# Sums of weight forms and channels from GpSimd to VectorE, and value stores from GpSimd's DMA queue to ScalarE's

## The chip, the cores and the metric

The kernel runs on one core of one Trainium2 chip. The metric is the time of one execution on the device in microseconds (us). The core has five engines that run their own instruction queues side by side: TensorE (PE in the profile; its weight loads are PEld), VectorE (DVE), ScalarE (ACT), GpSimd (POOL) and SyncE (SP), which here only issues DMA transfers. DMA transfers can be issued from the queues of SyncE, ScalarE and GpSimd; in this kernel nearly all come from SyncE.

## The reference

One layer of a streaming encoder works on two groups with the same weights: a prompt of 2048 frames and a sample of 32 frames, each frame 1024 channels wide, all in float32.

```python
h = rmsnorm(x, g_pre_mix)
z = h @ w_in                               # 1024 -> 2560: pool u | q | f | i | g
y_pool = pool_mix(u_ext, ...)              # trailing means over 2/4/8/16 frames, a map per group
q = silu(zq); fgate = lb + (1 - lb) * sigmoid(zf); kin = (1 - lb) * sigmoid(-zf)
S1, o = hgrn_run(S0, q, kin, zi, log(fgate))   # gated recurrence, 4 heads, chunks
y_hg = rmsnorm(o, g_hg_norm) * silu(zg)
x = x + rmsnorm(concat(y_pool, y_hg) @ w_out, g_post_mix)
h2 = rmsnorm(x, g_pre_ffn)
f = (silu(h2 @ w_gate) * (h2 @ w_up)) @ w_down   # 1024 -> 2816 -> 1024
x = x + rmsnorm(f, g_post_ffn)
```

The outputs are the new frames of both groups, the last 15 pooling rows and the recurrence's states.

## The kernel before, in words

The prompt is worked in two halves of 1024 frames (`halves[0]` and `halves[1]`; `S.B` is true for the second). For each half come the values (columns `i` of `w_in`), the other columns with the recurrence and the pooling windows, the projection by `w_out` (`project`), and the gate and up products (`gate_up`). The down products of both halves stand at the end (`down`).

Matmuls are exact to float32 by splitting. Every operand is stored as a rounded upper part (`hi`, float32r, by a ScalarE copy) and a lower part (`lo`, the difference, by a VectorE subtraction), and a product is three matmuls: hi by hi, hi by lo, lo by hi. Large products are also blocked 2x2 with seven products in place of eight. So each operand needs sums and differences of its blocks, called forms, before the split. The products are numbered 1 to 7; products 1 and 2 and 4 use plain blocks, and 5, 6, 7 and 3 use sums.

`weight_forms` makes the forms of the weights that the second half's columns use. It runs while TensorE works on the first half's gate and up products. For each of eight pairs of column blocks it loads four blocks (`weight_block`, tile `wb`, 128x512), makes four sums and differences on GpSimd, and splits four of the results (`put`): the upper part on ScalarE (line 464), the lower part on GpSimd (line 465), then two stores to the DRAM tile `wd` on SyncE's queue. `front_pairs` loads them back for the second half (line 929), three products ahead.

`second_channels` prepares the second half's channels: scaled inputs (line 575), their upper and lower parts (lines 577 to 581), and then block sums on 128x1024 tiles (line 373, the helper `sums`): `b12`, `t2s`, `b11` and `b21`, two tiles each. `t2s` is on VectorE, the three others on GpSimd.

`values` computes the second half's values into eight PSUM banks. Each is copied out to a tile `vt`, even ones by ScalarE and odd ones by VectorE (line 809), and stored to the DRAM tile `vd` from GpSimd's queue (line 810). The recurrence loads a head's part later (line 1192).

Right after the values comes `front_pairs`. For each pair, products 1, 2, 6, 7, 5, 4, 3 run in this order (banks `gx`, `gz`, `gy`). Product 1 is copied out by ScalarE (line 956), products 6, 5 and 3 accumulate further into the same bank `gx`, and line 967 copies the bank out between products 6 and 5, so product 5 must wait for that copy. `use` (lines 857 to 873) applies the sigmoids on ScalarE into tiles `sg` (lines 864, 868) and the products on VectorE. Line 956 is the first ScalarE instruction of a pair; 864 and 868 of `use` come ahead of 967 in the program.

What sets the order: the program is written out in full, and TensorE's order is the program's. Side work (weight forms, channels, recurrence) is written as generators, `Task`s. A `yield` of so many nanoseconds says how much planned TensorE time (`Pace.t`, added up by `mm`, line 205) must pass before the task's next step is put into the program, at the next `poll`, which stands after every third matmul of a product. `finish` puts all remaining steps at once; `second_start` calls it for the weight forms, eleven products before the end of the first half's gate and up, and then begins the second half's loads. On the other four engines a planner orders the instructions when the kernel is built, by its own costs and by program order as priority. Each engine then runs its queue strictly in order.

Tiles come from rotating pools. `t2` tiles (128x512) share 25 slots among all these stages: `wb`, `fhi`, `flo`, `vt`, `sg`, `wf`, `hhi`, `hlo`, `c11` and others. A new tile's first writer waits until the slot's former tile has been read for the last time, which for a stored tile means that the store has landed.

Of the kernel before, what the change touches and what calls it, by code (L numbers as in the profile page):

```python
# [13 lines left out]
ALU = mybir.AluOpType  # L14
# [20 lines left out]
T1 = 2000.0  # L35
Y0 = 18000.0
Y1 = 8000.0
FORMS = 8000.0
LOOKRAW = 2
SLOT = HALF  # L40
CHUNK = 128
# [43 lines left out]
def body(tc, ins, outs, cst):  # L85
    nc = tc.nc
    ctx = ExitStack()
    with ctx:
# [9 lines left out]
        def ztile(name, shape=None, dt=F32):  # L98
            return UP.tile(shape or [P, SLOT], dt, tag="u", name=name)

        def xtile(name, shape=None):
            return UP.tile(shape or [P, SLOT], F32R, tag="u", name=name)

        def mmbank(name="mmb"):
            return MM.tile([P, 512], F32, tag="mm", name=name)

        def axbank(name="axb"):
            return AX.tile([P, 512], F32, tag="ax", name=name)
# [4 lines left out]
        def t2(name, shape=None, dt=F32):  # L113
            return TP.tile(shape or [P, 512], dt, tag="t", name=name)
# [94 lines left out]
        def rcost(n):  # L209
            return max(107.0, n / 2.4 + 2.5)  # L210
# [74 lines left out]
        def ahead(n):  # L285
            its = Stream.items
            raws(n + LOOKRAW)
            while Stream.nsplit < min(n, len(its)):
                i = Stream.nsplit
                its[i] = split(its[i], Stream.wide[i])  # L290
                Stream.nsplit += 1

        def take(look=LOOK):
            i = Stream.used
            Stream.used += 1
            ahead(i + 1 + look)
            r = Stream.items[i]
            Stream.items[i] = None
            return r

        def in_turn(trios):

            for a, b in ((0, 2), (0, 3), (1, 2)) if len(trios) > 1 else ((0, 2), (1, 2), (0, 3)):
                for t in trios:
                    yield t[a], t[b]
# [57 lines left out]
        def form(src):  # L363
            hl = [(xtile("fhi", [P, D]), xtile("flo", [P, D])) for _ in src]
            for r, (hi, lo) in zip(src, hl):
                nc.scalar.copy(hi, r)
            for r, (hi, lo) in zip(src, hl):
                nc.vector.tensor_tensor(lo, r, hi.bitcast(F32), ALU.subtract)
            return hl

        def sums(dst, a, b, op, eng=nc.vector):
            for d, x, y in zip(dst, a, b):
                eng.tensor_tensor(d, x, y, op)
# [66 lines left out]
        vd = DP.tile([NH, P, NCH, P], F32, name="vd")  # L440
# [12 lines left out]
        def weight_block(n, m, kh):  # L453
            kind, h = PAIRS[n][m]
            c0 = COLS[kind] + h * P
            t = t2("wb", [P, 4, P])
            nc.sync.dma_start(out=t, in_=w_in[kh * 512:kh * 512 + 512, c0:c0 + P].rearrange("(k p) c -> p k c", p=P))
            return t.rearrange("p k c -> p (k c)")

        def weight_forms():  # L460

            def put(n, p, src):
                hi, lo = t2("fhi", dt=F32R), t2("flo", dt=F32R)
                nc.scalar.copy(hi, src)
                v.tensor_tensor(lo, src, hi.bitcast(F32), ALU.subtract)
                for i, t in enumerate((hi, lo)):
                    nc.sync.dma_start(out=wd[n][p - 1, :, i, :], in_=t.bitcast(F32))

            v = nc.gpsimd
            for n in range(len(PAIRS)):  # L470
                a21, a22 = weight_block(n, 1, 0), weight_block(n, 1, 1)
                yield FORMS
                v.tensor_tensor(a22, a21, a22, ALU.add)
                a11 = weight_block(n, 0, 0)
                yield FORMS
                put(n, 5, a22)
                v.tensor_tensor(a21, a11, a21, ALU.subtract)
                v.tensor_tensor(a11, a22, a11, ALU.subtract)
                a12 = weight_block(n, 0, 1)
                yield FORMS  # L480
                put(n, 7, a21)
                v.tensor_tensor(a12, a12, a11, ALU.subtract)
                yield FORMS
                put(n, 6, a11)
                yield FORMS
                put(n, 3, a12)

        class Half:
            pass
# [58 lines left out]
        def channel_loads(S):  # L548

            for tg in range(2):  # L550
                S.rb[tg] = t2("rb")
                nc.sync.dma_start(out=S.rb[tg], in_=roots[0:1, tg * 512:tg * 512 + 512].broadcast_to([P, 512]))
            S.xT = [[None] * 4 for _ in range(2)]
            for kp in range(2):
                channel_pair(S, kp)

        def channel_pair(S, kp):
            for tg in range(2):
                x = S.xT[tg][kp] = ztile("xT", [P, 2, 512])
                t0 = S.tok0 + tg * 512  # L560
                nc.sync.dma_start(out=x, in_=x_t[:, 2 * kp:2 * kp + 2, t0:t0 + 512])
            raws(Stream.used + kp + 1)

        def second_channels(S):

            channel_loads(S)
            yield Y0
            for kp in range(4):
                for tg in range(2):
                    x, rb = S.xT[tg][kp], S.rb[tg]  # L570
                    hi, lo = xtile("fhi", [P, D]), xtile("flo", [P, D])
                    parts = [slice(0, 512), slice(512, 1024)] if kp == 0 else [slice(0, 1024)]
                    S.xT[tg][kp] = flat = x.rearrange("p k t -> p (k t)")
                    for i in range(2):
                        nc.vector.scalar_tensor_tensor(x[:, i], x[:, i], g_pre[:, 2 * kp + i:2 * kp + i + 1], rb, ALU.mult, ALU.mult)
                        if kp == 0:
                            nc.scalar.copy(hi[:, parts[i]], flat[:, parts[i]])
                    if kp:
                        nc.scalar.copy(hi, flat)
                    for cs in parts:  # L580
                        nc.vector.tensor_tensor(lo[:, cs], flat[:, cs], hi[:, cs].bitcast(F32), ALU.subtract)
                    S.plain[tg].append((hi, lo))
                    if kp == 0 and tg == 0:
                        ahead(Stream.used + 1)
                S.seen[0] = 2 * kp + 2
                if kp < 2:
                    channel_pair(S, kp + 2)
                yield Y1
            b11, b21 = S.xT[0][0:2], S.xT[0][2:4]
            b12, b22 = S.xT[1][0:2], S.xT[1][2:4]  # L590
            S.F[1], S.F[2], S.F[3] = S.plain[0][0:2], S.plain[0][2:4], S.plain[1][2:4]
            sums(b12, b12, b11, ALU.subtract, nc.gpsimd)
            yield T1
            t2s = [ztile("t2s", [P, D]) for _ in range(2)]
            sums(t2s, b22, b12, ALU.subtract)
            yield 2000.0
            S.F[6] = form(t2s)
            sums(b11, t2s, b11, ALU.subtract, nc.gpsimd)
            yield 3000.0
            sums(b21, b21, t2s, ALU.subtract, nc.gpsimd)  # L600
            S.F[7] = form(b11)
            yield 3000.0
            S.F[5] = form(b12)
            yield 3000.0
            S.F[4] = form(b21)
# [186 lines left out]
        def values(S, pairs):  # L792
            pss = [mmbank("vps") for _ in range(4)] + [axbank("vps") for _ in range(4)]
            for k in range(0, KD, 2):
                _, hi, lo = take(1)
                while S.seen[0] < k + 2:
                    S.norm.step()
                if k == 4:
                    next(pairs)
                for i in range(8):  # L800
                    c0 = i % 4 * P
                    trios = [(*(x[:, kk * 512 + c0:kk * 512 + c0 + P] for x in S.plain[i // 4][k // 2]), hi[kk], lo[kk]) for kk in range(2)]
                    for n, (a, b) in enumerate(in_turn(trios)):
                        mm(pss[i], a, b, k == 0 and n == 0, k + 2 == KD and n == 5, rcost(512))
                        if n % 3 == 2:
                            poll()
                    if k + 2 == KD:
                        vt = t2("vt", [P, NH, P])
                        (nc.vector.tensor_copy if i % 2 else nc.scalar.copy)(vt, pss[i].rearrange("p (h c) -> p h c", c=P))
                        nc.gpsimd.dma_start(out=vd[:, :, i, :].rearrange("h p c -> p h c"), in_=vt)  # L810
            Smp.mix = Task(sample_mix(), 4000.0)

        def sample_values():
# [1301 lines left out]
```

## Time and profile before

| what | value |
|---|---|
| median of 3 runs | 2081.92 us (2081.21 to 2084.04) |
| the profiled execution's own time | 2080.79 us |
| its span, first to last instruction | 2079.0 us |
| mean granted TensorE clock | 0.995 |
| TensorE busy | 2050.9 us, 99% |
| VectorE busy | 1464.9 us, 70% |
| ScalarE busy | 850.8 us, 41% |
| GpSimd busy | 413.9 us, 20% |
| DMA | 389.15 MB, 187 GB/s on average |

The profile gives each instruction's start and duration on its engine, by line, operation and tile. A row of the lists of waits reads: engine, tile and line that waited, what ended the wait, the sum of the waits in us, how many, and the longest. In a timeline a bracket gives the engine's idle time ahead of an instruction and what ended it; "xN" is the number of instructions merged in the row. "Issue" there means that nothing which the profile shows ended the wait. Idle time of an engine other than the one that sets the end costs nothing by itself.

### The profile page before, as it was taken

How to read it: one execution, taken by the hardware profiler on the slowest of the kernel's cores; microseconds unless marked ns; L12 is line 12 of the kernel's file. 1: busy time of each engine (PE TensorE's matmuls, PEld its weight loads, DVE VectorE, ACT ScalarE, POOL GpSimd, SP SyncE). 2: the span in 40 equal slices, each digit the busy share in tenths (PEclk: the TensorE clock that was granted, in tenths of full speed). 3: DMA queues.
4: the chain of work that ended last, by engine and by line, in shares of the span. 5: the costliest groups of instructions: out<-in, count | busy, mean ns of one | idle time of the engine just before them, and what ended most of it. 6: DMA issues, size and time to landing. Idle time of an engine off the chain costs nothing.

```text
span 2079.0 us, 34579 instructions
## 1 busy us (share of the span) xinstructions
PE 2050.9 (99%) x12980; PEld 1669.0 (80%) x12980; DVE 1464.9 (70%) x2252; ACT 850.8 (41%) x1689; POOL 413.9 (20%) x484
## 2 busy tenths in 40 slices
PE   9999999999999999799999999999999999999998
PEld 8788888888888887678887788888888778888876
DVE  5555674799887888666676697776666766566587
ACT  6544344654554544333344563444444521011032
POOL 0223421212222221333242100000000210110134
PEclk9999999999999999899999999999999999999999
DMA  8633344537787778464573614554445797776779
GB/s 290 200 101 113 103 142 143 171 109 236 226 245 216 219 217 253 152 239 151 194 267 132 193 51 137 163 149 145 138 142 167 235 336 221 220 224 200 220 199 225
DMA packets 427672, 389.15 MB, mean 187 GB/s; under 512 B 22360, under 2 KB 324432, under 8 KB 427504
## 3 DMA queue, kind: packets, MB, share of 16 engines
q1 hardware_dynamic: 424288, 376.65, 57.7%
q0 software_dynamic: 2784, 9.70, 2.2%
q8 instruction: 103, 1.69, 0.3%
q14 instruction: 65, 0.53, 0.1%
q10 hardware_dynamic: 432, 0.57, 0.1%
HBM read 251.77 MB, written 135.07 MB: 186 GB/s over the span
## 4 chain that ended last, share of the span: by engine, by line
PE 93%; DVE 4%; issue 1%; ACT 1%; DMA 1%; POOL 1%; DVEq 0%; SPq 0%; ACTq 0%; POOLq 0%
PE gx L206 26%; PE gy L206 13%; PE dx L206 11%; PE ops L206 9%; PE mmb L206 8%; PE gz L206 6%; PE dy L206 5%; PE vps L206 4%; PE dz L206 3%; PE gb L206 1%; PE gw L206 1%; PE gsps L206 1%; PE tps L349 1%; PE ups L206 1%; DVE acc L1887 1%
## 5 line engine op out<-in xcount | busy, mean ns | idle before, releaser
L206 PE MATMUL gx<-fhi,wf 128*128 128x512 f32 x1632 | 464.5, 393 | 13.0 <-ACT c L967 11.4
L206 PEld LDWEIGHTS gx<-fhi,wf 128*128 128x128 f32 x1632 | 304.5, 188 | 78.6 <-ACT c L967 11.8
L206 PE MATMUL gx<-flo,wf 128*128 128x512 f32 x816 | 256.1, 393 | 0.0
L206 PE MATMUL gy<-fhi,wf 128*128 128x512 f32 x832 | 239.9, 391 | 1.0 <-DVE c L1709 1.0
L206 PE MATMUL dx<-dhi,hst 128*128 128x512 f32 x640 | 185.4, 391 | 0.8 <-DVE acc L1887 0.7
L206 PEld LDWEIGHTS gy<-fhi,wf 128*128 128x128 f32 x832 | 155.4, 188 | 33.4 <-ACT wf L1598 1.6
L206 PEld LDWEIGHTS gx<-flo,wf 128*128 128x128 f32 x816 | 153.8, 188 | 32.3
L1603 DVE TENSOR_TENSOR wf<-s,wf 128x512 fp32r<-128x512 f32 x176 | 136.7, 783 | 58.6 <-ACT wf L1598 57.1
L1887 DVE TENSOR_TENSOR acc<-dx,acc 128x512 f32<-128x512 f32 x168 | 115.0, 689 | 71.1 <-PE dx L206 70.2
L206 PEld LDWEIGHTS dx<-dhi,hst 128*128 128x128 f32 x640 | 119.6, 188 | 29.9 <-issue 3.4
L1598 ACT CAST wf<-s 128x512 fp32r<-128x512 f32 x176 | 107.0, 620 | 73.5 <-PE gy L206 17.4
L206 PE MATMUL gy<-flo,wf 128*128 128x512 f32 x416 | 131.1, 392 | 0.0
L1826 ACT CAST dhi<-t 128x1024 fp32r<-128x1024 f32 x20 | 20.6, 1054 | 252.8 <-DVE dlo L1827 183.9
L1813 POOL TENSOR_TENSOR t<-wdr 128x1024 f32<-128x1024 f32 (+1 forms) x6 | 13.4, 2226 | 514.3 <-DMA wdr<-in_w_down_dram 506.2
L1598 ACT CAST wf<-wraw 128x512 fp32r<-128x512 f32 x132 | 80.6, 621 | 79.2 <-PE gx L206 35.9
L206 PE MATMUL gz<-fhi,wf 128*128 128x512 f32 x384 | 112.5, 393 | 0.0
L1603 DVE TENSOR_TENSOR wf<-wraw,wf 128x512 fp32r<-128x512 f32 x132 | 94.4, 722 | 24.5 <-ACT wf L1598 24.3
L206 PE MATMUL dx<-dlo,hst 128*128 128x512 f32 x320 | 98.7, 390 | 0.0
L206 PE MATMUL dy<-dhi,hst 128*128 128x512 f32 x320 | 98.6, 389 | 0.0
L206 PEld LDWEIGHTS gy<-flo,wf 128*128 128x128 f32 x416 | 78.1, 188 | 16.9 <-issue 0.8
L206 PE MATMUL mmb<-hTlo,whi 128*128 128x512 f32 x256 | 90.1, 409 | 0.0
L1887 DVE TENSOR_TENSOR acc<-dy,acc 128x512 f32<-128x512 f32 x88 | 60.6, 689 | 38.6 <-PE dy L206 38.0
(381 smaller groups left out, 4153.2 us busy)
## 6 DMA issues: line engine op xcount, KB each, us to landing
hst<-hdFalse SPq DMA_DIRECT2D x140, 256.0 KB, 2.9
hst<-hdTrue SPq DMA_DIRECT2D x140, 256.0 KB, 3.6
wf<-wd SPq DMA_DIRECT2D x112, 256.0 KB, 5.1
wraw<-in_w_gate_dram SPq DMA_DIRECT2D x50, 512.0 KB, 4.3
wraw<-in_w_up_dram SPq DMA_DIRECT2D x50, 512.0 KB, 4.5
hdFalse<-hhi SPq DMA_DIRECT2D x77, 256.0 KB, 4.0
hdFalse<-hlo SPq DMA_DIRECT2D x77, 256.0 KB, 2.7
hdTrue<-hhi SPq DMA_DIRECT2D x77, 256.0 KB, 2.3
```

Of the source, the lines that this page charges most:

```text
L206: nc.tensor.matmul(out, l, r, start=start, stop=stop, skip_group_check=more)
L349: nc.tensor.transpose(ps[:, c:c + P], xn[:, (2 * kp + kk) * P:(2 * kp + kk + 1) * P], ident)
L1598: nc.scalar.copy(wf[:, 0], getattr(M, src) if isinstance(src, str) else src)
L1603: nc.vector.tensor_tensor(wf[:, 1], getattr(M, src) if isinstance(src, str) else src, wf[:, 0].bitcast(F32), ALU.subtract)
L1813: nc.gpsimd.tensor_tensor(W.t1, b12, b11, ALU.subtract)
L1826: nc.scalar.copy(hi, src)
L1887: nc.vector.tensor_tensor(dst, ps, dst, ALU.add)
```

## The change

Three things change, with no change in what is computed.

- In `weight_forms` the sums and the lower parts go from GpSimd to VectorE. `put` becomes a generator: it pauses 3000 ns between the upper part and the lower part with its stores. The pauses between the other steps go from 8000 to 5600 ns.
- In `second_channels` the three sums on GpSimd go to VectorE.
- In `values` the stores of `vt` to `vd` are issued from ScalarE's queue instead of GpSimd's.

```diff
-FORMS = 8000.0
+FORMS = 5600.0
...
             def put(n, p, src):
                 hi, lo = t2("fhi", dt=F32R), t2("flo", dt=F32R)
                 nc.scalar.copy(hi, src)
+                yield 3000.0
                 v.tensor_tensor(lo, src, hi.bitcast(F32), ALU.subtract)
                 for i, t in enumerate((hi, lo)):
                     nc.sync.dma_start(out=wd[n][p - 1, :, i, :], in_=t.bitcast(F32))
 
-            v = nc.gpsimd
+            v = nc.vector
...
-                put(n, 5, a22)
+                yield from put(n, 5, a22)
...
-                put(n, 7, a21)
+                yield from put(n, 7, a21)
...
-                put(n, 6, a11)
+                yield from put(n, 6, a11)
...
-                put(n, 3, a12)
+                yield from put(n, 3, a12)
...
-            sums(b12, b12, b11, ALU.subtract, nc.gpsimd)
+            sums(b12, b12, b11, ALU.subtract)
...
-            sums(b11, t2s, b11, ALU.subtract, nc.gpsimd)
+            sums(b11, t2s, b11, ALU.subtract)
...
-            sums(b21, b21, t2s, ALU.subtract, nc.gpsimd)
+            sums(b21, b21, t2s, ALU.subtract)
...
-                        nc.gpsimd.dma_start(out=vd[:, :, i, :].rearrange("h p c -> p h c"), in_=vt)
+                        nc.scalar.dma_start(out=vd[:, :, i, :].rearrange("h p c -> p h c"), in_=vt)
```

## The prediction

> **What bounds the kernel now.** First the top of the page, then TensorE's waits, then the stretch in which the longest of them lies.
>
> ```profile
> span 2079.0 us, 34579 instructions
> PE 2050.9 (99%) x12980; PEld 1669.0 (80%) x12980; DVE 1464.9 (70%) x2252; ACT 850.8 (41%) x1689; POOL 413.9 (20%) x484
> PE gx L206 <- ACT c L967: 11.4, 1, 11.4
> PE vps L206 <- DVE c L1727: 2.2, 1, 2.2
> PE gy L206 <- DVE c L1709: 1.0, 1, 1.0
> 850.00:900.00 50.00, 38.59 (x224) 29.69 (x223) 23.48 (x33) 15.82 (x25) 10.42 (x12) 0.86 0.61 206
> ```
>
> TensorE is busy for 99% of the span, so only its 28.1 us of idle time, and time at a lowered clock, can be won. One wait is 11.4 of them; it lies in the only stretch of the middle whose granted clock is low (0.86). The columns of the last row are the busy times of PE, PEld, DVE, ACT and POOL, the clock, the DMA engines' share and GB/s. Now this place on TensorE, ScalarE and GpSimd:
>
> ```profile
> 869.45 0.61 PE L206 MATMUL gy<-fhi,wf 128*128 128x512 f32 x2
> 881.48 1.22 PE L206 MATMUL gx<-fhi,wf 128*128 128x512 f32 x2 [11.41 <-ACT c L967]
> 861.98 0.59 ACT L956 COPY c<-gx 128x512 f32<-128x512 f32 x1 [3.02 <-DVE hs L1521]
> 877.00 1.28 ACT L864 ACT_TABLE_LOAD   x1 [14.42 <-DMA vd<-vt]
> 879.80 0.63 ACT L868 ACTIVATE sg<-c 128x512 f32<-128x512 f32 x1 [0.88 <-DMA vd<-vt]
> 880.84 0.58 ACT L967 COPY c<-gx 128x512 f32<-128x512 f32 x1
> 868.23 0.76 POOL L810 DMA_DIRECT2D vd<-vt  x1 [4.66 <-issue]
> 872.51 0.75 POOL L810 DMA_DIRECT2D vd<-vt  x1 [3.53 <-issue]
> 877.23 0.76 POOL L810 DMA_DIRECT2D vd<-vt  x1 [3.97 <-issue]
> vd<-vt POOLq DMA_DIRECT2D x8, 256.0 KB, 3.2
> ```
>
> This is the second half's first pair. TensorE stops at 870.07 (881.48 less 11.41) because bank `gx` may not be accumulated into until line 967 has copied it out. That copy stands on ScalarE behind the sigmoid of line 864, and the sigmoid's output tile waits 14.42 us for a slot that a values store still reads. The stores trickle: GpSimd issues them 4.3 and 4.7 us apart, "issue" naming no releaser, although one lands in 3.2 us and the DMA engines are 0.61 busy. So the chain is store queue, tile slot, sigmoid, copy, TensorE.
>
> ```profile
> 859.18 2.72 PE gx L206 x12
> 881.48 5.09 PE gx L206 x12
> 872.00:874.00 2.00, 0.00 (x0) 0.00 (x0) 0.00 (x0) 0.00 (x0) 0.75 (x1) 0.57 0.33 60
> ```
>
> After the stop, twelve matmuls take 5.09 us, not 2.72: 2.4 us more for the clock, which fell about 2.2 us into the idle time (0.57 over 872 to 874 is full speed for 0.3 of the 2 us, half after it).
>
> **The stores on ScalarE's queue.** Eight issues leave GpSimd and go on ScalarE, where each is queued behind its copy and, for odd tiles, waits for VectorE's copy. Behind it stand the next value copies, line 956, the sigmoid and line 967.
>
> ```profile
> L1916 ACTq DMA_DIRECT2D out_dram<-acc x2: 339/342/344, 2074.5 to 2075.8; - x2
> hdFalse<-hhi SPq DMA_DIRECT2D x77, 256.0 KB, 4.0
> 858.74 1.88 DVE L809 COPY vt<-vps 128x512 f32<-128x512 f32 x3
> 861.86 0.68 DVE L809 COPY vt<-vps 128x512 f32<-128x512 f32 x1
> ```
>
> An issue on ScalarE's queue took 0.34 us for 256 KB, so eight cost 2.7 us; ScalarE idles 3.02 us in front of line 956, which covers them. Without that cover they would cost TensorE 2.7 us. A hidden-tile store of the same size and pattern lands in 4.0 us on the other hardware queue. Taking VectorE no earlier than before, its last copy ends at 862.54, the last store is issued by 862.9 and lands by 866.9. Line 956 then ends near 863.5; TensorE needs it at 864.6 (859.18 and two products of 2.72). The sigmoid is free at 866.9. From the table load (877.00) to line 967 (880.84) is 3.84 us, of which 0.88 was a second wait for a store (879.80), so 2.96 without; line 967 starts at 869.9 and ends at 870.5, 0.4 us after TensorE asks for it. With VectorE earlier (below) the wait is nil. I take 0.5 us left, too short to lower the clock: **gain 11.4 + 2.4 - 0.5 = 13.3 us**. The bounds are 13.8 and, by the second rival, 7.1.
>
> **The channels' sums on VectorE.** Six 128x1024 operations move.
>
> ```profile
> 809.52 2.56 DVE L575 SCALAR_TENSOR_TENSOR xT<-xT,cons,rb 128x512 f32<-128x512 f32 x1
> 812.61 0.73 DVE L575 SCALAR_TENSOR_TENSOR xT<-xT,cons,rb 128x512 f32<-128x512 f32 x1
> 836.74 2.35 DVE L373 TENSOR_TENSOR t2s<-xT 128x1024 f32<-128x1024 f32 x2
> 843.57 3.42 DVE L368 TENSOR_TENSOR flo<-t2s,fhi 128x1024 fp32r<-128x1024 f32 x1
> 846.91 11.31 DVE L368 TENSOR_TENSOR flo<-xT,fhi 128x1024 fp32r<-128x1024 f32 x6
> ```
>
> On VectorE such an operation costs 2.35 / 2 = 1.18 us, so six cost 7.1. But VectorE is itself stretched wherever GpSimd computes: 2.56 against 0.73 (1.8 lost), 3.42 against 1.18 (2.2), six in 11.31 against 7.1 (4.2). These 8.2 us come back, so VectorE reaches the value copies about 1 us earlier. For TensorE this is slack, except at the 2.2 us wait at the start of the values (`vps`), which is a VectorE backlog. There the gain is at most 1.8; the loss at most two sums less that, 0.5, and what the forms' late end adds (next). I take nothing.
>
> **The weight forms on VectorE.** Per pair four sums and four lower parts move, 64 operations in all.
>
> ```profile
> 455.00:785.00 330.00, 328.98 (x1452) 272.21 (x1451) 281.60 (x385) 164.10 (x296) 93.30 (x67) 1.00 0.74 226
> 1250.00:1580.00 330.00, 330.00 (x1966) 272.45 (x1965) 232.59 (x375) 142.41 (x258) 0.00 (x0) 1.00 0.50 147
> 445.74 2.14 POOL L473 TENSOR_TENSOR wb<-wb 128x512 f32<-128x512 f32 x1 [41.97 <-DVE s L1574]
> 758.24 1.29 POOL L473 TENSOR_TENSOR wb<-wb 128x512 f32<-128x512 f32 x1 [7.62 <-DMA hdFalse<-hhi]
> 793.84 0.75 DVE L575 SCALAR_TENSOR_TENSOR xT<-xT,cons,rb 128x512 f32<-128x512 f32 x1 [2.65 <-DMA rb<-roots]
> ```
>
> The two rows are the same gate and up products of the two halves, with GpSimd at 93.3 us and at nothing. A VectorE operation takes 281.60 / 385 = 0.731 us in the first and 0.620 in the second: 385 x 0.111 = 43 us come back, and 64 x 0.620 = 40 us are added. VectorE's load stays at 279 of 330 us, under TensorE, and the wait of 1.0 us for line 1709 may go or stay. Even with no relief 281.60 + 40 would stay under 330. The bounds for TensorE are a gain of 1.0 and, where VectorE also waits beside its work, the loss of the third rival; I take nothing, since the relief is measured.
>
> The planned time per pair stays 40 us (5 x 8 before; 5 x 5.6 + 4 x 3 now), but each pause is rounded up to the next poll. A pair takes (758.24 - 445.74) / 7 = 44.6 us. 40 planned are 42.0 real, since line 209 plans a matmul at 0.2158 us and twelve take 2.72; the other 2.6 are 0.5 for each of five pauses. Nine pauses take 2 us more, and the last pair falls 14 us later. `forms.finish()` then writes out more at once, about two operations and one pair of stores more. The stores stand on SyncE ahead of the second half's first loads, on which VectorE already waits 2.65 us at 793.84. At worst that wait doubles and 2.65 us reach TensorE at the start of the values: the other end for that term.
>
> **Sum.** 13.3 us. The profiled execution took 2080.79 us (span 2079.0 and 1.8 around it), which gives 2067.5; the median of the runs is 1.1 higher, 2081.92, which gives **2068.6**.
>
> **Rivals.** (1) The stores come no faster, since the same transfers run. For it: nothing in the rows says what GpSimd's issue waits for. Against: 4.3 us apart with the engines 0.61 busy, and 3.2 to land. Then only a few tenths move: 2081.5. The Trainium skill, DMA: Bandwidth & Descriptors, "Issuing engines are not separate DMA queues", speaks for this rival: all queues run on the same 16 engines, so issuing elsewhere saves only sequencer time. By that rule, the gap between issues would not close; the trace's gaps speak against it here.
>
> (2) ScalarE takes the wait over.
>
> ```profile
> SPq L1530 <- DVE hlo L1528: 45.8, 9, 14.2
> SPq L929 <- DMA xwv<-in_w_in_dram: 0.4, 2, 0.2
> 858.85 0.36 SPq L1530 DMA_DIRECT2D hdFalse<-hlo  x1
> ```
>
> SyncE's queue is held 14.2 us until 858.85, and its transfers sometimes wait for unrelated ones (second row). Were the first store on ScalarE to wait for that transfer's landing (858.85 + 0.36 + 4.0 = 863.2), then eight issues (2.7) and four value copies of 0.59 (as line 956's) follow, line 956 ends at 868.9, 4.3 us late, and such a stop lowers the clock again, 2.4. The gain is 13.8 - 6.7 = 7.1: 2074.8. Against it: VectorE gives that lower part earlier without GpSimd beside it.
>
> (3) Slower: VectorE waits in order for the blocks of weights.
>
> ```profile
> POOL wb L482 <- DMA wb<-in_w_in_dram: 22.5, 5, 6.3
> POOL wb L473 <- DMA wb<-in_w_in_dram: 15.1, 3, 6.0
> POOL wb L477 <- DMA wb<-in_w_in_dram: 10.6, 4, 4.6
> L1573 DVE TENSOR_TENSOR s<-wraw 128x512 f32<-128x512 f32 x16 | 11.0, 685 | 3.9 <-DMA wraw<-in_w_up_dram 3.7 <-issue 0.2
> ```
>
> GpSimd sat out 48.2 us in twelve such waits; the lead shrinks from 8 to 5.6 us, which makes 48.2 + 12 x 2.4 = 77. On VectorE, whose other operations then queue behind, 51 us are free (330 - 279), 26 reach TensorE: 2081.9 - 13.3 + 26 = 2095. It decides from 51 + 13 = 64 us of waiting on. Against it: VectorE fills a load's time with other work, and waited only 3.7 us for the comparable loads of line 1573.
>
> **How the numbers follow.** My sum 0.64; the second rival, and milder forms of it, 0.18; the first 0.08; the third 0.10. Less than 0.2% (4.2 us) this measurement cannot tell from no change. The sum and the second rival lie below 2077.8: faster 0.82, same 0.08, slower 0.10. The range begins where the 13.8, the 2.2 and 1.0 us waits and about 2 us of smaller ones are all gone, 2063, and reaches over the second rival with 2.65 more lost at the start of the values (2077.4), to 2078; the first and the third rival, 0.18, are left out.
>
> **What would show it.** TensorE's list without line 967, or under 1 us; value stores on ScalarE's queue within some 12 us, ending near 863; no clock dip near 872; VectorE near 279 us over the first half's gate and up, at about 0.62 us per operation; the wait of `vps` between 0.4 and 5. I am wrong if the stores still lie 4 us apart, if ScalarE stands at line 810 or 956, or if VectorE idles on `wb`.

## The result, and the profile after

The changed kernel takes 2062.23 us (median of 5 runs, 2061.62 to 2063.02) against 2081.92 us before (5 runs, 2080.48 to 2084.04): a ratio of 0.9906, 95% interval 0.9892 to 0.9919, which is 19.7 us. The forecast was 2068.6 us and its range ended at 2063.0, so the kernel gained more than was forecast, and 0.8 us more than the range held.

The top of the page of the changed kernel, and then the list of TensorE's waits:

```profile
span 2059.8 us, 34464 instructions
PE 2047.2 (99%) x12980; PEld 1666.4 (81%) x12980; DVE 1455.6 (71%) x2322; ACT 851.9 (41%) x1689; POOL 293.1 (14%) x406
```

```profile
PE idle L206 <- POOL ones L149: 1.0, 1, 1.0
PE yps L1083 <- DVE on L1076: 0.9, 1, 0.9
PE gx L206 <- DMA wf<-wd: 0.7, 1, 0.7
PE dx L206 <- DVE acc L1888: 0.6, 2, 0.4
PE gb L206 <- ACT xz L845: 0.4, 1, 0.4
PE gy L206 <- DVE c L1710: 0.3, 1, 0.3
```

Lines after 465 have a number higher by one now: 957, 968 and 1710 are the 956, 967 and 1709 of before. The wait of 11.4 us for the copy between products 6 and 5 is gone, so is the one of 2.2 us at the start of the values (`vps`), and the one of 1.0 us at line 1709 is 0.3. TensorE is idle for 12.6 us of its span where it was 28.1, and busy for 3.7 us less.

ScalarE's and its queue's rows around the former stop, in the timeline of the changed kernel, and the stores' row in the list of DMA issues:

```profile
846.62 0.38 ACTq L811 DMA_DIRECT2D vd<-vt  x1
...
849.53 0.93 ACTq L811 DMA_DIRECT2D vd<-vt  x2
...
854.77 1.83 ACTq L811 DMA_DIRECT2D vd<-vt  x2
...
858.24 0.59 ACT L957 COPY c<-gx 128x512 f32<-128x512 f32 x1 [0.97 <-PE gx L206]
858.84 1.28 ACT L865 ACT_TABLE_LOAD   x1
861.75 0.63 ACT L865 ACTIVATE sg<-c 128x512 f32<-128x512 f32 x1 [1.63 <-DVE c L960]
...
863.68 0.59 ACT L968 COPY c<-gx 128x512 f32<-128x512 f32 x1 [0.26 <-PE gx L206]
```

```profile
vd<-vt ACTq DMA_DIRECT2D x8, 256.0 KB, 2.6
```

All eight stores are issued within 10 us (846.6 to 856.6), and the median time to landing is 2.6 us. The table load waits for no store any more (14.42 us before). Line 968 now waits for TensorE, not TensorE for it.

VectorE in the same stretch, and then two windows of the changed kernel (PE, PEld, DVE, ACT and POOL busy with their counts, the clock, the DMA share, GB/s), and the second window of the kernel before:

```profile
842.52 4.63 DVE L368 TENSOR_TENSOR flo<-xT,fhi 128x1024 fp32r<-128x1024 f32 x4
...
848.80 0.69 DVE L810 COPY vt<-vps 128x512 f32<-128x512 f32 x1
...
855.52 0.69 DVE L810 COPY vt<-vps 128x512 f32<-128x512 f32 x1 [0.70 <-PE vps L206]
```

```profile
455.00:785.00 330.00, 329.67 (x1454) 272.40 (x1453) 277.46 (x448) 163.97 (x296) 2.17 (x4) 1.00 0.75 227
785.00:900.00 115.00, 115.00 (x795) 92.66 (x796) 91.96 (x138) 49.87 (x76) 10.41 (x15) 1.00 0.79 253
```

```profile
785.00:900.00 115.00, 100.78 (x496) 80.53 (x495) 81.67 (x97) 43.95 (x64) 28.68 (x18) 0.94 0.67 216
```

Four lower parts take 4.63 us, 1.16 each, where six took 11.31, 1.89 each. VectorE's copies of values begin at 848.80 instead of 858.74, and the later ones wait for TensorE. In the stretch from 785 to 900 TensorE is busy throughout.

Setting the two traces side by side, matmul by matmul, shows where the 19.2 us of span came from: 1.0 up to 800 us (the wait at line 1709 lies there), 2.5 at the start of the values, 13.7 from the stop to the end of the low clock behind it, and 2.0 in small pieces after that. The remaining 0.5 is outside the span or between the profiled run and the median.

### The profile page after: what moved, and what is told of

It reads as the page before. It is cut to its first block, busy times and chain, and to the rows that moved or that the text cites. A ratio compares the mean times of both kernels' runs of the same rounds, so it can differ in the third digit from the quotient of the medians.

```text
span 2059.8 us, 34464 instructions
## 1 busy us (share of the span) xinstructions
PE 2047.2 (99%) x12980; PEld 1666.4 (81%) x12980; DVE 1455.6 (71%) x2322; ACT 851.9 (41%) x1689; POOL 293.1 (14%) x406
## 4 chain that ended last, share of the span: by engine, by line
PE 92%; DVE 4%; ACT 1%; issue 1%; DMA 1%; POOL 1%; SPq 0%; DVEq 0%; POOLq 0%; ACTq 0%
PE gx L206 26%; PE gy L206 13%; PE dx L206 10%; PE ops L206 9%; PE mmb L206 8%; PE gz L206 6%; PE dy L206 5%; PE vps L206 4%; PE dz L206 3%; PE gb L206 1%; PE gw L206 1%; PE gsps L206 1%; DVE acc L1888 1%; PE tps L349 1%; PE ups L206 1%
## 5 line engine op out<-in xcount | busy, mean ns | idle before, releaser
L1604 DVE TENSOR_TENSOR wf<-s,wf 128x512 fp32r<-128x512 f32 x176 | 120.2, 687 | 53.8 <-ACT wf L1599 52.9
L1604 DVE TENSOR_TENSOR wf<-wraw,wf 128x512 fp32r<-128x512 f32 x132 | 89.6, 687 | 26.2 <-ACT wf L1599 26.0
L1814 POOL TENSOR_TENSOR t<-wdr 128x1024 f32<-128x1024 f32 (+1 forms) x6 | 13.4, 2229 | 514.5 <-DVE hs L1519 405.6
```

The costliest lines, as they stand in the source:

```text
L1604: nc.vector.tensor_tensor(wf[:, 1], getattr(M, src) if isinstance(src, str) else src, wf[:, 0].bitcast(F32), ALU.subtract)
L1814: nc.gpsimd.tensor_tensor(W.t1, b12, b11, ALU.subtract)
```

## The experiments

Each ratio is to the kernel before, timed beside the run, with a median between 2081.3 and 2082.2 us; the 95% interval stands in brackets. First the parts of the change are taken alone, and then left out one at a time.

**The stores alone.** Kernel before with one line changed.

```diff
-                        nc.gpsimd.dma_start(out=vd[:, :, i, :].rearrange("h p c -> p h c"), in_=vt)
+                        nc.scalar.dma_start(out=vd[:, :, i, :].rearrange("h p c -> p h c"), in_=vt)
```

> The kernel before with the value stores alone on ScalarE's queue. Theory (the store queue made the stop): the stop of 11.4 us and its 2.4 us of lowered clock go, 2081.9 - 13.8 = 2068; the wait of the values' start (2.2 us) and the one of 1.0 us at line 1709 stay. Rival (the stop needs VectorE and GpSimd relieved as well): ScalarE stands behind VectorE's late value copies, at most half goes, 2075 or more.

Measured: 2071.33 us, ratio 0.9953 (0.9937 to 0.9970). The stop at line 967 is gone, but TensorE has a new one. Its two longest waits, then ScalarE's and VectorE's rows in this kernel's timeline:

```profile
PE vps L206 <- DVE c L1727: 2.2, 1, 2.2
PE gx L206 <- ACT c L956: 2.2, 1, 2.2
```

```profile
855.19 5.20 ACTq L810 DMA_DIRECT2D vd<-vt  x2
860.48 0.59 ACT L809 COPY vt<-vps 128x512 f32<-128x512 f32 x1 [5.32 <-DVE vt L809]
...
866.71 0.58 ACT L956 COPY c<-gx 128x512 f32<-128x512 f32 x1
```

```profile
847.48 11.30 DVE L368 TENSOR_TENSOR flo<-xT,fhi 128x1024 fp32r<-128x1024 f32 x6
...
859.31 1.87 DVE L809 COPY vt<-vps 128x512 f32<-128x512 f32 x3
```

The second store in the queue is that of a tile which VectorE copies. VectorE reaches it only at 859.31, behind six stretched lower parts, and until then ScalarE stands still. Line 956 runs at 866.71, 4.7 us later than in the kernel before (861.98). This is the second rival's effect, by another late tile than the one it named.

**The sums alone.** Kernel before with the three sums on VectorE.

```diff
-            sums(b12, b12, b11, ALU.subtract, nc.gpsimd)
+            sums(b12, b12, b11, ALU.subtract)
...
-            sums(b11, t2s, b11, ALU.subtract, nc.gpsimd)
+            sums(b11, t2s, b11, ALU.subtract)
...
-            sums(b21, b21, t2s, ALU.subtract, nc.gpsimd)
+            sums(b21, b21, t2s, ALU.subtract)
```

> The kernel before with the channels' sums alone on VectorE. Theory (GpSimd's sums stretch VectorE): the 2.2 us wait of the values' start shrinks, the stop of line 967 stays at about 11 us, 2079 to 2081. Rival (the stores wait for VectorE, not for their own queue): the stop shrinks by the microsecond or more by which the value copies come earlier, and the stores lie closer, 2075 or less.

Measured: 2073.79 us, ratio 0.9964 (0.9951 to 0.9977): 8.2 us, for a part that the prediction put at nothing. TensorE's longest wait, GpSimd's first and last stores, and VectorE's first copy in this kernel:

```profile
PE gx L206 <- ACT c L967: 4.9, 1, 4.9
```

```profile
849.16 1.02 POOL L810 DMA_DIRECT2D vd<-vt  x1 [61.88 <-ACT vt L809]
...
875.00 0.76 POOL L810 DMA_DIRECT2D vd<-vt  x1 [2.09 <-issue]
```

```profile
851.14 0.67 DVE L809 COPY vt<-vps 128x512 f32<-128x512 f32 x1
851.74 2.34 DVE L368 TENSOR_TENSOR flo<-xT,fhi 128x1024 fp32r<-128x1024 f32 x2
```

The stores trickle as before, but they begin 5.8 us earlier (849.16 against 854.93). TensorE itself is only some 1.4 us ahead here. The first store waits for ScalarE's first copy of values, and on ScalarE that copy stands behind the upper parts of the sums (line 366). ScalarE's rows, first in the kernel before and then in this one:

```profile
849.27 4.85 ACT L366 CAST fhi<-xT 128x1024 fp32r<-128x1024 f32 x5 [5.09 <-POOL xT L373]
854.02 1.07 ACT L809 COPY vt<-vps 128x512 f32<-128x512 f32 x2
```

```profile
842.75 4.97 ACT L366 CAST fhi<-xT 128x1024 fp32r<-128x1024 f32 x5 [2.62 <-DVE xT L373]
848.24 0.59 ACT L809 COPY vt<-vps 128x512 f32<-128x512 f32 x1 [0.52 <-PE vps L206]
```

Before, ScalarE waits 5.09 us for a sum on GpSimd, whose last four sums take 2.85 to 5.06 us each; with the sums on VectorE, at 1.17 us each, its first copy comes 5.8 us earlier and waits for TensorE. VectorE's first copy is earlier too, and stands ahead of the last two lower parts. So the trickle reaches less far into the first pair, and the stop is 4.9 us instead of 11.4.

**The weight forms alone.** Kernel before with the edits to `weight_forms` and `FORMS` alone.

```diff
-            v = nc.gpsimd
+            v = nc.vector
```

> The kernel before with the weight forms alone on VectorE, with the new pauses. Theory (the forms on GpSimd stretch VectorE): VectorE's mean operation over the first half's gate and up falls from 0.73 to about 0.62 us, the wait of 1.0 us at line 1709 goes, the stop of line 967 stays; 2079 to 2081. Rival (VectorE is filled by the added work and by waits for the blocks): new waits of TensorE in that stretch, 2082 or more.

Measured: 2079.89 us over 10 runs, ratio 0.9992 (0.9982 to 1.0001), not told apart from no change. The stop of 11.2 us stays; the 2.2 us wait of `vps` goes, although the sums are still on GpSimd; VectorE has 276.98 us of work from 455 to 785.

**Everything but the stores.** Changed kernel, stores on GpSimd again.

```diff
-                        nc.scalar.dma_start(out=vd[:, :, i, :].rearrange("h p c -> p h c"), in_=vt)
+                        nc.gpsimd.dma_start(out=vd[:, :, i, :].rearrange("h p c -> p h c"), in_=vt)
```

> The changed kernel with the value stores back on GpSimd's queue; GpSimd has nothing else to do there. Theory (the queue itself is slow): the stores still lie about 4 us apart and the stop of line 967 stays near 11 us, with the small waits gone: 2062.2 + 13.8 = 2076. Rival (GpSimd's sums and the stretched VectorE made the stores late): the stop goes or falls under 5 us, 2068 or less.

Measured: 2073.83 us, ratio 0.9962 (0.9947 to 0.9977). The trickle is back and stops TensorE for 6.7 us at line 968. On top of the rest the stores are worth 11.6 us.

**Everything but the sums.** Changed kernel, the three sums on GpSimd again.

```diff
-            sums(b12, b12, b11, ALU.subtract)
+            sums(b12, b12, b11, ALU.subtract, nc.gpsimd)
...
```

> The changed kernel with the channels' sums back on GpSimd. Theory (ScalarE's queue is only as early as VectorE's value copies, which GpSimd's sums delay): line 956 comes some 2 us late again as with the stores alone, and the stores end near 866 instead of 857; 2067 to 2070. Rival (with the stores off GpSimd's queue the sums cost nothing where they are): 2064 or less.

Measured: 2068.58 us, ratio 0.9937 (0.9919 to 0.9955). TensorE's two longest waits and a window behind the first of them in this kernel:

```profile
PE gx L206 <- ACT c L957: 2.1, 1, 2.1
PE vps L206 <- DVE c L1728: 1.8, 1, 1.8
```

```profile
866.00:867.00 1.00, 1.00 (x3) 0.81 (x3) 0.49 (x1) 0.99 (x2) 0.00 (x0) 0.50 1.09 379
```

The sums are worth 6.4 us on top of the rest. Against the changed kernel's trace, 2.1 us are lost at the start of the values, 2.5 at line 957, and 2.4 behind it, where the clock is at half.

**Everything but the weight forms.** Changed kernel with `weight_forms`, `put` and `FORMS` as before.

```diff
-            v = nc.vector
+            v = nc.gpsimd
```

> The changed kernel with the weight forms back on GpSimd with the old pauses; sums on VectorE and stores on ScalarE's queue. Theory (the forms are worth the small waits at line 1709 and at the start of the values only): those come back, no wait at lines 956 and 967, 2064 to 2066. Rival (the forms on VectorE also make the rest of the order better): 2068 or more.

Measured: 2065.56 us, ratio 0.9921 (0.9907 to 0.9936), runs from 2062.55 to 2067.87. No stop at the first pair; the wait at line 1709 is 2.4 us. The forms are worth 3.3 us by the medians, most of it at that wait; the interval of this ratio and that of the changed kernel (0.9892 to 0.9919) overlap, so the size is not firm.

**The stores on SyncE.** Changed kernel, the stores on the other hardware queue.

```diff
-                        nc.scalar.dma_start(out=vd[:, :, i, :].rearrange("h p c -> p h c"), in_=vt)
+                        nc.sync.dma_start(out=vd[:, :, i, :].rearrange("h p c -> p h c"), in_=vt)
```

> The changed kernel with the value stores on SyncE's queue instead of ScalarE's. Theory (any queue that issues in 0.4 us will do): stores under 1 us to issue, no stop at line 968, 2062 to 2064. Rival (SyncE stands in order behind other waits, the longest 11 us for a lower part): stores and the loads behind them late, a stop of 2 us or more, 2066 or more.

Measured: 2062.82 us, ratio 0.9912 (0.9897 to 0.9928), the same as the changed kernel, without a stop. It matters that the stores leave GpSimd's queue, not that they go to ScalarE's.

**Longer runs of bytes in the stores, still from GpSimd.** Kernel before with `vd` laid out so that a store writes 128 runs of 2 KB instead of 512 of 512 bytes; the later load of a head then reads the shorter runs.

```diff
-        vd = DP.tile([NH, P, NCH, P], F32, name="vd")
+        vd = DP.tile([NCH, P, NH, P], F32, name="vd")
...
-                        nc.gpsimd.dma_start(out=vd[:, :, i, :].rearrange("h p c -> p h c"), in_=vt)
+                        nc.gpsimd.dma_start(out=vd[i], in_=vt)
...
-                nc.sync.dma_start(out=vh, in_=vd[h])
+                nc.sync.dma_start(out=vh, in_=vd[:, :, h, :].rearrange("i p c -> p i c"))
```

> The kernel before with the DRAM tile of the values laid out so that a store writes 128 runs of 2 KB instead of 512 runs of 512 bytes (and a head's load reads runs of 512 bytes), still on GpSimd's queue. Theory (GpSimd's issue waits for room for its descriptors, 512 per store): a quarter of the descriptors, issues 1 to 2 us apart where they were 2.9 to 6, the stop of line 967 small, 2068 to 2073. Rival (each issue waits for the store before to land, whatever its descriptors): issues 3 us apart or more, the stop as before, 2079 or more.

Measured: 2071.97 us, ratio 0.9952 (0.9934 to 0.9970). GpSimd's stores in this kernel, and their row among the DMA issues:

```profile
858.37 0.81 POOL L810 DMA_DIRECT2D vd<-vt  x1 [2.33 <-ACT vt L809]
863.17 3.77 POOL L810 DMA_DIRECT2D vd<-vt  x7 [4.00 <-DVE vt L809]
```

```profile
vd<-vt POOLq DMA_DIRECT2D x8, 256.0 KB, 3.9
```

With the same queue, the same bytes and a median landing time no shorter (3.9 us against 3.2), seven issues follow each other 0.54 us apart, and the stop at line 967 is gone. So an issue on GpSimd's queue need not wait for the landing of the store ahead. In the kernel before it does wait for it. The median of 3.2 us hides this. These are the landing times of the single stores issued at 868.23, 872.51 and 877.23 there:

```profile
DMA to landing us min/median/max: 4.0/4.0/4.0
DMA to landing us min/median/max: 4.4/4.4/4.4
DMA to landing us min/median/max: 2.5/2.5/2.5
```

The first lands at 872.2, and the next issue starts at 872.51; that one lands at 876.9, and the next starts at 877.23; that lands at 879.8, and the next starts at 880.08. Each issue follows the landing of the store ahead by 0.30 us. This holds for all of the last six issues of the kernel before, and for all seven that follow the first one in the run with the sums alone. So with 512 runs to a store each issue waits for the store ahead to land, and with 128 longer runs it does not. That fits room for descriptors which one such store fills and which comes free as it lands, as the theory had it; the traces show no such room, so this reason is not shown. On ScalarE's queue stores of 512 runs do not wait like this: two are issued within 0.93 us (849.53 in the changed kernel).

It was not VectorE either: a window of the kernel before, between two of its slow issues, has VectorE (third column) doing nothing for 3.9 us.

```profile
873.30:877.20 3.90, 0.00 (x0) 0.00 (x0) 0.00 (x0) 0.20 (x1) 0.00 (x0) 0.50 0.84 264
```

The Trainium skill, SBUF — State Buffer, "SBUF: two separate sides", names a cause for slow stores from GpSimd's queue: GpSimd writes their descriptors and is locked out while VectorE holds the port that they share. Its remedy, another engine's queue, is what worked; its cause cannot be the one in this window, since VectorE was idle.

**GpSimd work beside VectorE, first try.** Changed kernel with 256 extra multiplications of a constant tile on GpSimd, which nothing reads.

```diff
+        def beside():
+            for _ in range(4):
+                nc.gpsimd.tensor_tensor(ones, ones, ones, ALU.mult)
...
                 v.tensor_tensor(lo, src, hi.bitcast(F32), ALU.subtract)
+                beside()
```

> The changed kernel with work added on GpSimd that nobody waits for: at each place where a weight form's operation was, four multiplications of a 128x128 tile of ones with itself (256 in all). Theory (GpSimd's two-input operations slow VectorE's): VectorE's busy time over 455 to 785 us rises from 277 us by 15 us or more, its mean operation from 0.62 us to 0.65 or more, and some of the small waits return; 2062.5 to 2066. Rival (the stretched operations were an effect of the order only): mean 0.62 us, 2062.2.

Measured: 2151.91 us, ratio 1.0339 (1.0323 to 1.0355). It says nothing on the question. The operations depend on nothing, so they ran from 13.9 us on, ahead of GpSimd's other work at the start, and TensorE waited 69.9 us there. The next two runs tie the extra work to the tiles.

**GpSimd work beside the weight forms.** Changed kernel; GpSimd multiplies, for each result that VectorE writes, its four 128x128 blocks into a tile that nothing reads.

```diff
+        def beside(t, n):
+            for c in range(0, n, P):
+                nc.gpsimd.tensor_tensor(ones, t[:, c:c + P], t[:, c:c + P], ALU.mult)
...
                 v.tensor_tensor(a22, a21, a22, ALU.add)
+                beside(a22, 512)
```

> The changed kernel with work added on GpSimd at the weight forms: behind each of the 64 operations moved to VectorE, four multiplications on GpSimd (128x128 each, reading what VectorE has just written, into a tile that nobody reads). VectorE's own work is the same. Theory (GpSimd's two-input operations slow VectorE's): VectorE's busy time over 455 to 785 us rises from 277 us towards 300 or more, its mean operation from 0.62 us to 0.67 or more, and the waits at line 1709 and at the start of the values come back; 2063.5 to 2067. Rival (they do not share anything; the stretched operations came from the order): busy time 277 us, 2062.2.

Measured: 2066.61 us, ratio 0.9924 (0.9909 to 0.9939); the profile is of the fastest execution, 2063.12 us. The window of the first half's gate and up, and TensorE's longest wait:

```profile
455.00:785.00 330.00, 328.07 (x1447) 271.07 (x1446) 299.61 (x445) 164.26 (x295) 160.71 (x241) 1.00 0.74 225
```

```profile
PE gy L206 <- DVE c L1719: 1.9, 2, 1.6
```

A VectorE operation takes 299.61 / 445 = 0.673 us beside this work and 277.46 / 448 = 0.619 without it, and TensorE's wait at the same place as before (line 1709 there, 1719 here) is back. VectorE is stretched by GpSimd's presence, though less than by the wider operations before (0.731).

**GpSimd work beside the channels' sums.** The same with 48 multiplications that read the sums.

```diff
             sums(b12, b12, b11, ALU.subtract)
+            for b in b12:
+                beside(b, D)
```

> The changed kernel with work added on GpSimd at the channels' sums: behind each pair of sums sixteen multiplications on GpSimd (128x128 each, reading the sums, into a tile that nobody reads), 48 in all. Theory (GpSimd's work beside VectorE delays the value copies, and ScalarE's store queue with them): VectorE's 128x1024 lower parts before the values take 1.4 us or more each instead of 1.15, the value copies come 2 us or more later, and a wait of up to 2 us for line 957 comes back; 2062.5 to 2066. Rival (the sums' place in the order made the difference): 2062.2, lower parts at 1.15 us.

Measured: 2062.82 us, ratio 0.9909 (0.9894 to 0.9924), no different from the changed kernel. VectorE's and GpSimd's rows:

```profile
844.41 4.62 DVE L368 TENSOR_TENSOR flo<-xT,fhi 128x1024 fp32r<-128x1024 f32 x4
```

```profile
833.14 43.74 POOL L567 TENSOR_TENSOR ones<-xT 128x128 f32<-128x128 f32 x48 [276.19 <-DVE xT L373]
```

The expectation of my theory fell here. VectorE's lower parts take 1.16 us each, as without the work, and it is GpSimd that is slow: it is busy for 40.1 us of this row, 0.84 us an operation, against 0.67 beside the weight forms. Before, six 128x1024 sums on GpSimd stretched the same lower parts to 1.89. Whether the width of GpSimd's operation decides which of the two engines gives way was not tried with wide operations beside the changed kernel; it stays open.

**The pauses of before.** Changed kernel with `FORMS = 8000.0` and without the pause of 3000 ns in `put`.

```diff
-FORMS = 5600.0
+FORMS = 8000.0
...
-                yield 3000.0
...
-                yield from put(n, 5, a22)
+                put(n, 5, a22)
```

> The changed kernel with the old pauses: all forms on VectorE, the lower part in the same step as the upper part, 8000 ns between the steps. Theory (the planner fills VectorE with other work until the upper part is there, so the pause costs and gains nothing): 2062 to 2063.5. Rival (without the pause VectorE stands waiting for ScalarE's upper part, in order): waits of VectorE at the lower parts' line of 15 us or more in all, new waits of TensorE, 2065 or more.

Measured: 2061.49 us (2060.99 to 2062.59), ratio 0.9902 (0.9885 to 0.9918). VectorE waits 13.4 us in 13 places for the upper parts at line 464, and TensorE has no wait for it. Putting the lower parts a step later is worth nothing that these runs can tell. The runs overlap with those of the changed kernel, so it is not shown to be faster either.

**What makes line 956 late when the stores move alone.** Two kernels: the one before with only the stores moved, to SyncE's queue; and with them on ScalarE's queue, and all value copies on ScalarE.

```diff
-                        nc.gpsimd.dma_start(out=vd[:, :, i, :].rearrange("h p c -> p h c"), in_=vt)
+                        nc.sync.dma_start(out=vd[:, :, i, :].rearrange("h p c -> p h c"), in_=vt)
```

> The kernel before with the eight stores of values on SyncE's queue, the sums and the weight forms left on GpSimd. Theory (with the sums on GpSimd, VectorE's value copies are late; stores on ScalarE's queue then hold ScalarE itself 5.3 us at the second store, and that is the 2.2 us wait of TensorE for the copy of line 956 with the stores alone): ScalarE is not held here, line 956 runs near 862 as in the kernel before instead of 866.7, the 2.2 us wait goes, no stop at line 967; about 2069 us, 2 us under the stores alone (2071.3). Rival (the 2.2 us has another cause, or is traded for a late load of weight forms on SyncE's queue): 2071 us or more.

```diff
-                        (nc.vector.tensor_copy if i % 2 else nc.scalar.copy)(vt, pss[i].rearrange("p (h c) -> p h c", c=P))
-                        nc.gpsimd.dma_start(out=vd[:, :, i, :].rearrange("h p c -> p h c"), in_=vt)
+                        nc.scalar.copy(vt, pss[i].rearrange("p (h c) -> p h c", c=P))
+                        nc.scalar.dma_start(out=vd[:, :, i, :].rearrange("h p c -> p h c"), in_=vt)
```

> The kernel before with the stores of values on ScalarE's queue and all eight value copies of line 809 on ScalarE, none on VectorE. Theory: ScalarE waits for nothing but its own copies, eight of 0.6 us and eight issues of 0.4 us; line 956 runs before 866 and TensorE's wait of 2.2 us there goes; banks come free in order; 2068 to 2070 us. Rival (ScalarE's own load makes line 956 late, not VectorE's copies): the wait at line 956 stays near 2 us and the time at 2071 us.

Measured: 2072.01 us, ratio 0.9956 (0.9942 to 0.9970), and 2067.70 us, ratio 0.9932 (0.9919 to 0.9944). TensorE's two longest waits in the first, and line 956 in the second:

```profile
PE vps L206 <- DVE c L1727: 2.2, 1, 2.2
PE gy L206 <- ACT hhi L1525: 2.0, 1, 2.0
```

```profile
863.84 0.58 ACT L956 COPY c<-gx 128x512 f32<-128x512 f32 x1
```

In both TensorE no longer waits for line 956. With all copies on ScalarE its row is at 863.84 instead of 866.71, and the time is 3.6 us under that of the stores alone, 0.3 below the range expected: it was VectorE's late copies that held ScalarE. On SyncE the time did not fall, as the rival there had it. SyncE's queue is now held by late copies too: it waits 8.5 us for ScalarE's first one, which stands behind the upper parts of GpSimd's sums. A little later TensorE loses 2.0 us at another wait, with the clock falling behind it; that this wait comes from the stores is not shown. So with the sums left on GpSimd the queue that takes the stores is held by value copies that the sums make late.

## Why the prediction was right or wrong

**The stop at line 967: right.** The chain of store queue, tile slot, sigmoid, copy and TensorE held. The trace gives 13.7 us for it, clock included, where the sum had 13.3; the stores ended at 856.6, not 863, and the 0.5 us left became nothing. One reading of it was wrong: "although one lands in 3.2 us" took the median for stores that landed in 4.0 and 4.4 us, each just ahead of the next issue.

**The stores need no help from VectorE: wrong.** The step "Taking VectorE no earlier than before, its last copy ends at 862.54, the last store is issued by 862.9 [...] Line 956 then ends near 863.5" counted when the last store can be issued, but not that ScalarE waits in order behind its second store already, with its own copies and line 956 behind that. Line 956 ended at 867.3 in the run that had the stores alone. That cost 2.2 us of TensorE, and the part alone gave 10.7 us instead of 13.3.

**The sums at nothing: wrong, and this is the step that failed.** It reads "These 8.2 us come back, so VectorE reaches the value copies about 1 us earlier. For TensorE this is slack", and then "I take nothing". Two rows of the kernel before were not counted in the 8.2:

```profile
819.27 2.55 DVE L1528 TENSOR_TENSOR hlo<-hs,hhi 128x512 fp32r<-128x512 f32 x1
...
840.75 2.90 DVE L1528 TENSOR_TENSOR hlo<-hs,hhi 128x512 fp32r<-128x512 f32 x1
```

Such a lower part takes 0.68 us alone, so they lose 1.9 and 2.2 us more, and 12.3 come back against 7 added: 5 us, not 1. In the run with the sums alone the last lower part ends at 854.08, with a copy ahead of it, instead of 858.22. The prediction also followed the sums only on VectorE: on ScalarE their upper parts held the first value copy, which came 5.8 us earlier with the sums moved. Nor was any of this slack. The queue of stores waits for these copies, and leaving the sums out costs 6.4 us. The wait at the start of the values, for which the prediction knew a gain of up to 1.8 us and took nothing, gave 2.5 us; it falls to 0.4 with the sums alone, but it goes with the weight forms alone as well, so it cannot be put down to the sums only.

**The weight forms on VectorE: right in load, wrong in worth.** 279 us were forecast for VectorE and 277.5 measured, at 0.619 us an operation against 0.62. But the bound of the gain was "a gain of 1.0" and nothing was taken; leaving the forms out costs 3.3 us by the medians, a size that is not firm (in that kernel the wait at line 1709 is 2.4 us). The loss of up to 2.65 us at the start of the values did not come.

**The sum and the range.** The low end, 2063, was put together from the 13.8, the waits of 2.2 and 1.0 us and "about 2 us of smaller ones"; the trace has 13.7, 2.5, 1.0 and 2.0. So the case that happened was the one written down as the edge. Against the 13.3 of the sum 6.4 us are missing: 2.5 at the start of the values, 1.0 up to 800 us and 2.0 in small pieces, all three put at nothing, 0.4 at the stop, and 0.5 outside the traces. That leaving out the sums costs 6.4 too is chance, since by the traces most of that lies at line 957 and in the clock behind it, where the 13.3 counted no loss. Singly left out, stores, sums and forms are worth 11.6, 6.4 and 3.3 us, together 21.3 for a gain of 19.7.

**The rivals.** The first fell: on ScalarE's or SyncE's queue, or with fewer and longer runs on GpSimd's, the stop is gone. It had more behind it than the prediction saw, since on GpSimd's queue the landings do set the pace; the prediction's "the trace's gaps speak against it here" does not hold, because each gap is a landing time and 0.30 us. The rule cited for it, from the Trainium skill, DMA: Bandwidth & Descriptors, "Issuing engines are not separate DMA queues", holds that another issuer saves only the sequencer's time; here another issuer saved 11.6 us. The second was real without the sums, by VectorE's copy rather than by SyncE's transfer, at 2.2 us, or 4.9 where the clock fell behind it, and absent with them. The third fell: VectorE waited 6.0 us in all for `wb` (3.8 at line 474, 2.2 at 478), of the 64 from which it would have decided.

## What to carry to other kernels

Put a price on an engine's earliness by listing every stretched row in the stretch, and then follow who waits for that engine, and who waits for the moved results; a queue that takes stores from two producers waits in order for the slower one. When several parts of a change act on the same place, price them together: here the stores could not give their full worth until the sums had made VectorE's copies early. Where GpSimd's DMA issues lie several microseconds apart with "issue" as the only reason, lay each issue beside the landing of the transfer ahead of it, one by one and not by the median, and try longer runs of bytes or another queue.

## What the hardware showed that was not expected

GpSimd's issues of 256 KB were 2.8 to 5.4 us apart at 512 runs of bytes, the last six of the kernel before each 0.30 us behind the landing of the store ahead, and 0.54 us apart at 128 runs, with median landing times of 3.2 and 3.9 us.

After a stop of about 2 us the clock may fall or not. It fell behind the 2.1 us stop in the kernel with everything but the sums (the window of 866 to 867 above, 0.50), and not behind the 2.2 us stop with the stores alone:

```profile
868.00:869.00 1.00, 1.00 (x6) 0.82 (x5) 0.13 (x1) 0.99 (x2) 0.00 (x0) 1.00 1.09 355
```

The traces tell more. In the middle of a kernel a stretch at half clock lasts 3.41 us or a multiple of it: 865.60 to 869.01 with everything but the sums, 872.29 to 885.95 in the kernel before. So in these traces the clock changes in steps of 3.41 us. With everything but the sums, the step that ends at 865.60 holds 2.0 us of the stop (TensorE idles from 863.58). With the stores alone, counted in such steps from the clock's first rise at 6.07, a border falls at 866.23, within the stop (865.18 to 867.35), and the steps on its two sides hold only 1.0 and 1.1 us of idle time. Counted like this in all the kernels here, between 450 and 2000 us, the clock fell after each of the eight steps at full clock with 1.93 us of idle time or more, and after none with 1.76 or less.

The Trainium skill, TensorE: Matmul & The Clock Gate, "What's actually happening", has a free-running window of about 3.4 us, and lets the clock fall after a whole idle window. The steps agree with the window; that 2.0 us of idle time within one were enough does not agree with a whole window without work.

The same operation on GpSimd beside VectorE took 0.667 us (160.71 / 241) in one stretch, with VectorE slowed from 0.619 to 0.673, and 0.84 us in another, with VectorE's lower parts not slowed.
